# Second-layer weights and last-stage factors requested by ScalarE in a queue of its own

## The chip, the core and the metric

The kernel runs on one core of a Trainium2 chip. Its engines are TensorE (PE in the profile), VectorE (DVE), ScalarE (ACT), GpSimd (POOL) and SyncE (SP); 16 DMA engines move data between the memory off the core (DRAM) and the on-chip buffers. The metric is the device time of one execution in microseconds (us): the median of three runs before is 2799.62 us, the lowest 2792.89, the highest 2799.96.

## The reference, cut to what matters

One inference step of a two-layer decoder, for a prompt of 2048 positions and 32 sample positions, width 1024. The first layer is gated linear attention. The second is attention over a sliding window of 128 positions, with 32 query heads in four groups that share one key and value head each, a gate, and an output projection:

```
q, gate = split(rmsnorm(h) @ b_w_in)          # 1024 -> 2048 + 2048
q = rope(rmsnorm(q per head))
o = attend(q, k_p, v_p, sinks)                # blocks of 128 queries
h = h + (o * silu(gate)) @ b_w_out            # 2048 -> 1024
```

`k_p, v_p` are projected once, from the residual stream after layer 0.

## The kernel before

A product of full precision is made of three f16 products of high and low halves, so each weight is held as a pair of f16 tiles. During layer 0 the kernel converts the weights of layer 1 into such pairs and writes them to DRAM: `Unit.prepare` (L247) writes the tensors called `pre`, and `form_steps` (L857) writes seven factors `wf0` to `wf6`, out of which the last stage makes the output projection of two blocks at a time with seven products in place of eight.

Layer 1 runs over four groups of heads (g), in each over 16 blocks of 128 positions (c): 64 iterations n = 16 g + c, and three more in which the pipeline runs empty. An iteration does three things woven together by the string `ORDER` (L1526): the projections of block n ("f" stands for one of 24 steps, TensorE's filler), the scores of block n-2 ("A", four of them, two heads each) and the values of block n-3 ("B", two of them). The order of TensorE's instructions is pinned from L1525 on; on the other engines a scheduler sets it when the kernel is built, by when it believes each instruction to be ready. After it is set, each engine and each DMA queue works strictly in it.

Between scores and values stands a chain: VectorE takes the minimum (L1281), ScalarE takes exponentials (L1286) and the high half (L192), VectorE the low half (L193), and SP's queue turns the result round with a DMA transposition into the buffers `sth` (heads 0, 1, 4, 5 of the group) and `pst` (heads 2, 3, 6, 7) at L1289, which the values read. SP's queue also holds the transposition of the queries (`X<-qe`, L1245), that of the output (`og<-ogT`, L638) and its store (`oge<-og`, L639), and the load of keys and values (`gl<-KVd`, L1233): some eight to eleven requests in an iteration.

In the same queue of SP stand the requests that the change touches, 64 of 512 KB each:

- `W<-pre` (L267, `Unit.fetch`), 36 of them: the prepared weights, four for keys and values, and eight for each group (four for the queries, four for the gate). They go into a ring of 12 buffers `W` (`NW`).
- `W<-wf` (L1542, `wform`), 12: factors 3, 4 and 5, into the same ring.
- `uT<-wf` (L1537, `wform_big`), 16: factors 0, 1, 2 and 6, a quarter each, into buffers `uT`.

The eight requests of the next group are traced at the end of iteration c = 12 (L1726). The scheduler moved them: it placed each where it believed the buffer free. A DMA request counts on one of eight semaphores that all requests of SP and ScalarE share in turn, so a request also waits until the last one that had the same semaphore, some eight requests back, has landed.

Of the kernel before, what the change touches and what calls it, by code (L numbers as in the profile page):

```python
# [22 lines left out]
NCH = SEQ // P  # L23
# [5 lines left out]
NKV = 4  # L29
# [35 lines left out]
def build(tc, i, o):  # L65
    nc = tc.nc
    ctx = ExitStack()
    with ctx:
        cp = ctx.enter_context(tc.tile_pool(name="cp", bufs=1))
        sb = ctx.enter_context(tc.tile_pool(name="sb", bufs=2))  # L70
        ps = ctx.enter_context(tc.tile_pool(name="ps", bufs=1, space=PSUM))
        dr = ctx.enter_context(tc.tile_pool(name="dr", bufs=1, space=DRAM))
        _body(tc, nc, cp, sb, ps, dr, i, o)


def _body(tc, nc, cp, sb, ps, dr, i, o):
# [6 lines left out]
    def T(tag, shape, dt, bufs=None):  # L83
        return sb.tile(shape, dt, tag=tag, name=nm(tag), **({} if bufs is None else {"bufs": bufs}))
# [22 lines left out]
    def later(dst, src, q=nc.sync):  # L107

        tc.keep_in_program_order(q.dma_start(dst, src))
# [31 lines left out]
    wfd = [dr.tile([P, 8, 2, 512], F16, tag=f"wf{n}", name=f"wf{n}") for n in range(7)]  # L141
# [17 lines left out]
    def run(steps):  # L159
        for f in steps:  # L160
            f()
# [39 lines left out]
    class Unit:  # L201
# [62 lines left out]

        def fetch(self):
            self.t = T("W", [P, 2, 1024], F16, NW)
            nc.sync.dma_start(self.t, self.pre)  # L267

        def __call__(self, k, hl, s):
            return self.t.rearrange("p z (k c) -> p z k c", c=self.ncol)[:, hl, k, s]  # L270
# [582 lines left out]
    gw = [GroupW(g) for g in range(NKV)]  # L853
# [677 lines left out]
    def wform_big(n, x, box={}):  # L1531

        if x == 0:
            t = box[n] = T("uT", [P, 8, 2, 512], F16, 4)
            wf[n] = lambda k, hl, s=ALL: t[:, k, hl, s]
        ks = slice(2 * x, 2 * x + 2)
        nc.sync.dma_start(box[n][:, ks], wfd[n][:, ks])  # L1537

    def wform(n, x, ts={}):

        t = ts[n, x] = T("W", [P, 2, 2, 512], F16, NW)
        nc.sync.dma_start(t, wfd[n][:, 2 * x : 2 * x + 2])  # L1542
        wf[n] = lambda k, hl, s=ALL: ts[n, k // 2][:, k % 2, hl, s]

    quarters = lambda f, n: [lambda x=x: f(n, x) for x in range(4)]
# [140 lines left out]
    def s_out(half):  # L1686

        cols = [slice(z * P, (z + 1) * P) for z in range(4)]
        right = [k + 2 for k in UP]
        fs, kts = ((0, 2, 5), UP + UP + right) if half else ((0, 3), UP + right)  # L1690
        return out_sample([lambda k, hl, z=z: wf[fs[k // 8]](k % 8, hl, z) for z in cols], half, b_finish_s, kts, OSCB)

    for t in range(-3, NKV * NCH):
        fill = []
        n = t + 3
        if n < NKV * NCH:
            g, c = divmod(n, NCH)
            blk = BBlk(g, c, gw[g])
            fill = blk.steps()
            parts[n] = blk.attend_steps()  # L1700
            if c == (SMC if g + 1 < NKV else 0):
                sm = SampleB(g, gw[g])
                boundary += [lambda sm=sm: run(sm.proj_steps())] + sm.steps()
        elif n < NKV * NCH + 3:
            fill = (pairs[0].steps(0) + pairs[0].steps(1), pairs[1].steps(0) + pairs[1].steps(1), s_out(0) + pairs[0].steps(2))[n - TOT]
        lists = {
            "A": list(parts[t + 1][0]) if t + 1 in parts else [],
            "B": list(parts.pop(t)[1]) if t in parts else [],
        }
        nf = ORDER.count("f")  # L1710
        seen = done = 0
        for x in ORDER:
            if x == "f":
                seen += 1
                upto = len(fill) * seen // nf
                run(fill[done:upto])
                done = upto
                if trickle and seen % 3 == 0:
                    trickle.pop(0)()
                if boundary and seen == 7 and n > TOT - NCH + 3:  # L1720
                    boundary.pop(0)()
                if summing and seen % 6 == 3 and (n > TOT or seen > 12):
                    summing.pop(0)()
            elif lists[x]:
                lists[x].pop(0)()
        if n < NKV * NCH and c == 12:  # L1726
            if g + 1 < NKV:
                run(gw[g + 1].steps())
        if n == TOT - 11:
            t_ = T("uT", [P, 8, 8, P], F16, 4)  # L1730
            for x in range(4):
                pr = pairs[x // 2]
                pr.l[x % 2] = [t_[:, 2 * x], t_[:, 2 * x + 1]]
                if x < 2:
                    pr.r[x] = pr.l[x]
                pr.fetch(x % 2, pr.l[x % 2])
        if n in (TOT - 7, TOT - 4):
            run(quarters(wform_big, {TOT - 7: 0, TOT - 4: 2}[n]))
        if n == TOT - 14:
            run(quarters(wform, 3))  # L1740
        if n == TOT - 1:
            trickle += [lambda x=x: pairs[0].load(x) for x in (3, 2)] + quarters(wform_big, 1)
            summing += pairs[0].sums()
        if n == TOT:
            trickle += quarters(wform, 4) + quarters(wform, 5)
        if n == TOT + 1:
            trickle += quarters(wform_big, 6)
        if boundary:
            boundary.pop(0)()
# [3 lines left out]
    for p_ in range(NCH // 2):  # L1753
# [8 lines left out]
        if p_ in (3, 4):  # L1762
            n = p_ - 3
# [87 lines left out]
```

## Time and profile before

| | us |
|---|---|
| median of 3 runs | 2799.62 |
| lowest and highest | 2792.89 and 2799.96 |
| the profiled execution, whole | 2794.24 |
| its span, first to last instruction | 2792.4 |
| TensorE busy in the span | 2700.0 (97%) |
| VectorE, ScalarE, GpSimd busy | 1701.5, 1391.9, 1134.0 |
| mean granted TensorE clock | 0.991 |

The profile comes from one execution with the hardware profiler on. "Busy" is the time in which an engine has an instruction under way. A view of windows gives, for a stretch of the span, the busy time of each engine (instructions in brackets), then the granted clock of TensorE, the mean busy share of the 16 DMA engines (which can pass 1, since an engine can have two packets under way) and the rate. A view of waits gives what an engine waited for in its idle time. A timeline gives start and duration of instructions, equal ones that follow each other as one row ("x12"), and in square brackets how long the engine was idle before and what released it. "SPq" and "ACTq" are requests: their duration is the time that the engine takes to issue them, not that of the transfer.

### The profile page before, as it was taken

The numbers are of one execution on the slowest core, as the hardware profiler recorded it, in microseconds if no ns is written. First come the engines' busy times: TensorE is split into PE (matmuls) and PEld (weight loads), VectorE is DVE, ScalarE is ACT, GpSimd is POOL, SyncE is SP. The second block draws the span as 40 slices with busy tenths as digits, with TensorE's granted clock in tenths as the row PEclk, the third lists the DMA queues.
The fourth block names the chain that finished last, engine by engine and source line by source line (L and its number), as shares of the span: only waits on it lengthen the run. The fifth ranks groups of instructions, "written<-read, shape, count | busy, mean of one in ns | idle before, by whom it ended". The sixth has DMA issues, their size and how long they took to land.

```text
span 2792.4 us, 51853 instructions
## 1 busy us (share of the span) xinstructions
PE 2700.0 (97%) x19266; PEld 1384.8 (50%) x19266; DVE 1701.5 (61%) x3474; ACT 1391.9 (50%) x3245; POOL 1134.0 (41%) x1604
## 2 busy tenths in 40 slices
PE   6899999999999999999999999999999999989999
PEld 4444544544454444445444555555555555544444
DVE  5655665666667564446413656677777767777653
ACT  6554655555556554433313555566666666651110
POOL 2342233322433231126305676666667657530000
PEclk9999999999999999999999999999999999999999
DMA  8462444433434454789846778978978889896431
GB/s 213 92 149 55 105 115 125 110 106 103 135 107 115 115 168 121 227 252 295 245 160 155 131 155 154 230 131 158 198 136 153 178 168 186 171 223 200 151 103 58
DMA packets 814470, 429.53 MB, mean 154 GB/s; under 512 B 649600, under 2 KB 723144, under 8 KB 814184
## 3 DMA queue, kind: packets, MB, share of 16 engines
q1 hardware_dynamic: 801256, 390.49, 59.8%
q0 software_dynamic: 10880, 35.66, 3.6%
q8 instruction: 150, 2.46, 0.4%
q14 instruction: 104, 0.85, 0.1%
q10 hardware_dynamic: 2080, 0.07, 0.0%
HBM read 178.75 MB, written 107.54 MB: 103 GB/s over the span
## 4 chain that ended last, share of the span: by engine, by line
PE 65%; ACT 9%; DMA 9%; DVE 7%; issue 5%; POOL 5%; SPq 1%; ACTq 0%; POOLq 0%; DVEq 0%
PE pj L102 39%; PE o L102 12%; PE tr L102 10%; PE kv L102 3%; ACT o L1286 2%; DMA pst<-v 2%; PE lev L102 1%; DVE v L193 1%; ACT v L192 1%; DMA wraw<-in_a_w_in_dram 1%; DMA pre<-pst 1%; DMA W<-in_state_gla_dram 1%; DVE o L1281 1%; POOL ogT L190 1%; DVE lev L1281 1%
## 5 line engine op out<-in xcount | busy, mean ns | idle before, releaser
L102 PE MATMUL pj<-W,uT 128*128 128x512 f16 x5088 | 1196.9, 380 | 6.9 <-ACT sg L500 2.5
L102 PEld LDWEIGHTS <-uT 128*128 128x128 f16 x6976 | 649.9, 98 | 697.5 <-issue 20.8
L102 PE MATMUL tr<-W,uT 128*128 128x512 f16 x1536 | 365.5, 379 | 0.0
L102 PEld LDWEIGHTS <-X 128*128 128x128 f16 x2744 | 184.6, 98 | 140.9 <-issue 9.9
L1286 ACT ACTIVATE o<-o,mx 128x256 f32<-128x256 f32 (+1 forms) x384 | 168.7, 439 | 166.7 <-DVE mx L1281 161.1
L181 POOL TENSOR_SCALAR rs_m<-ss 128x1 f32<-128x1 f32 (+3 forms) x190 | 43.6, 230 | 496.0 <-DVE ss L1183 184.2
L102 PE MATMUL pj<-uT,W 128*128 128x512 f16 (+1 forms) x912 | 189.3, 357 | 26.9 <-DMA uT<-ogT 23.9
L1281 DVE CUSTOM_DVE_ANT_0 o<-o,madd,nsink 128x256 f32<-128x256 f32 (+1 forms) x384 | 183.9, 479 | 43.5 <-PE o L102 39.2
L193 DVE SCALAR_TENSOR_TENSOR v<-o,v 128x512 f16<-128x512 f32 (+1 forms) x192 | 128.9, 672 | 104.6 <-ACT v L192 102.1
L182 POOL TENSOR_TENSOR rs_r<-rs_m,mhalf 128x1 f32<-128x1 f32 (+2 forms) x186 | 186.9, 1005 | 14.1
L533 POOL TENSOR_TENSOR KQ<-KQ,bt 128x256 f32<-128x256 f32 x112 | 99.9, 892 | 227.7 <-DVE X L190 222.4
L102 PEld LDWEIGHTS <-W 128*128 128x128 f16 x2448 | 129.9, 99 | 114.8 <-issue 23.0
L102 PEld LDWEIGHTS <-v 128*128 128x128 f16 x976 | 95.2, 98 | 115.7 <-issue 2.3
L190 POOL TENSOR_TENSOR ogT<-og,ogT 128x512 f16<-128x512 f32 x68 | 83.7, 1232 | 125.7 <-ACT ogT L189 120.6
L189 ACT ACTIVATE X<-KQ 128x512 f16<-128x512 f32 x128 | 84.6, 661 | 84.6 <-PE lev L102 61.1
L102 PEld LDWEIGHTS <-sg 128*128 128x128 f16 x800 | 77.7, 98 | 93.4 <-issue 1.2
L102 PE MATMUL o<-gl,X 128*128 128x256 f16 (+1 forms) x768 | 113.5, 270 | 7.6 <-DMA X<-qe 3.6
L192 ACT ACTIVATE v<-o 128x512 f16<-128x512 f32 (+1 forms) x192 | 111.2, 579 | 3.5
L190 DVE TENSOR_TENSOR X<-KQ,X 128x512 f16<-128x512 f32 x128 | 98.2, 767 | 21.2 <-ACT X L189 19.7
L1286 ACT ACTIVATE lev<-lev,mx 128x256 f32<-128x256 f32 (+1 forms) x128 | 56.5, 441 | 104.8 <-DVE mx L1281 102.8
L396 POOL TENSOR_TENSOR bt<-bt 128x256 f32<-128x256 f32 (+6 forms) x112 | 46.5, 416 | 146.5 <-ACT bt L385 139.5
L259 POOL DMA_DIRECT2D pre<-pst x72 | 50.4, 703 | 133.5 <-DVE pst L193 109.4
(439 smaller groups left out, 4871.1 us busy)
## 6 DMA issues: line engine op xcount, KB each, us to landing
pre<-pst POOLq DMA_DIRECT2D x72, 256.0 KB, 3.7
W<-pre SPq DMA_DIRECT2D x36, 512.0 KB
ogd<-ogk SPq DMA_DIRECT2D x68, 256.0 KB
wraw<-in_a_w_in_dram SPq DMA_DIRECT2D x64, 256.0 KB
wraw<-in_b_w_in_dram SPq DMA_DIRECT2D x64, 256.0 KB
oge<-og SPq DMA_DIRECT2D x64, 256.0 KB
wraw<-in_a_w_out_dram SPq DMA_DIRECT2D x32, 256.0 KB
X<-in_x_prompt_dram SPq DMA_DIRECT2D x32, 256.0 KB
```

The source lines that it names most:

```text
L102: return order(nc.tensor.matmul(*a, **k))
L181: pool.tensor_scalar(m[:n, :k], ss, a, b, ALU.mult, ALU.add)
L182: pool.tensor_tensor(r[:n, :k], m[:n, :k], mhalf[:n, :k], ALU.pow)
L189: act(hi, src, AF.Copy)
L190: eng.tensor_tensor(lo, src, hi, ALU.subtract)
L192: put(act(hi, src, AF.Copy, scale=sc))
L193: dve.scalar_tensor_tensor(lo, src, sc, hi, ALU.mult, ALU.subtract)
L259: nc.gpsimd.dma_start(self.pre[:, :, half * 512 : half * 512 + 512], t)
L396: pool.tensor_tensor(dst, two[:, :, 0], two[:, :, 1], ALU.mult)
L533: pool.tensor_tensor(keys, keys, d[:, :, 1:2].to_broadcast([P, NB, m]), ALU.mult)
L1281: dve.tensor_tensor_reduce(pm[:, z], pm[:, z], madd.rearrange("p a b -> p (a b)")[:, (2 - nk) * P :], -0.125, nsink[:, g * GRP + h : g * G ...
L1286: act(pm[:, z], pm[:, z], AF.Exp, scale=-1.0, bias=nm_[:, h : h + 1], accum_out=bx["sum"][:, h : h + 1])
```

## The change

The three places that request prepared data call `later(..., nc.scalar)`, a helper that stands in the kernel already (L107). It issues the request on the given engine, here ScalarE, and pins it behind what was traced on that engine before it. The place of the group requests in the code changes too: four at the end of iteration c = 12, the other four in iteration c = 15 after filler steps 15, 17, 19 and 21.

```diff
         def fetch(self):
             self.t = T("W", [P, 2, 1024], F16, NW)
-            nc.sync.dma_start(self.t, self.pre)
+            later(self.t, self.pre, nc.scalar)
...
         ks = slice(2 * x, 2 * x + 2)
-        nc.sync.dma_start(box[n][:, ks], wfd[n][:, ks])
+        later(box[n][:, ks], wfd[n][:, ks], nc.scalar)
...
         t = ts[n, x] = T("W", [P, 2, 2, 512], F16, NW)
-        nc.sync.dma_start(t, wfd[n][:, 2 * x : 2 * x + 2])
+        later(t, wfd[n][:, 2 * x : 2 * x + 2], nc.scalar)
...
+                if n < NKV * NCH - NCH and c == NCH - 1 and seen in (15, 17, 19, 21):
+                    nextg.pop(0)()
...
-        if n < NKV * NCH and c == 12:
-            if g + 1 < NKV:
-                run(gw[g + 1].steps())
+        if n < NKV * NCH - NCH and c == 12:
+            nextg = gw[g + 1].steps()
+            run(nextg[:4])
+            del nextg[:4]
```

Three places show how the built order moves. The first is SP's queue in the last iteration of group 0, from the output's transposition on; `W` are the weight buffers, `KVd`, `out_cvp` and `out_ckp` stores of keys and values. Before:

```order
L267 DMA W_18853<-pre_173 128x2048
L267 DMA W_18855<-pre_174 128x2048
L639 DMA oge_118<-og_19374 512x1x256
L267 DMA W_18857<-pre_175 128x2048
L1245 DMA_TRANSPOSE X_19388<-qe_19385 128x8x128
L267 DMA W_18859<-pre_176 128x2048
L1289 DMA_TRANSPOSE sth_19423<-v_19411 128x8x128
L1212 DMA KVd_15341<-w_3205_19454 512x1x128
L267 DMA W_18861<-pre_177 128x2048
L1224 DMA out_cvp_dram<-E_19470 128x256
```

And now:

```order
L639 DMA oge_118<-og_19366 512x1x256
L1245 DMA_TRANSPOSE X_19380<-qe_19377 128x8x128
L1289 DMA_TRANSPOSE sth_19415<-v_19403 128x8x128
L1212 DMA KVd_15341<-w_3201_19446 512x1x128
L1224 DMA out_cvp_dram<-E_19462 128x256
```

The weight requests are gone from between SP's own, and the rest stands as it did. Twelve stood here before (`pre_173` to `pre_184`: group 1's eight, and group 2's first four, whose buffers come free at the same time); the eight of group 1 now stand on ScalarE in this iteration.

The second place is ScalarE at the end of iteration 28 (g = 1, c = 12), behind the gate's activation; `qe` is the queries' high half, `Sh` a tile of the sample positions, `o` the scores, `es` the sink's exponential. Before:

```order
L1237 ACTIVATE sg_22576<-tr_22486 128x512
L1454 ACTIVATE Sh_22604<-tr_22595 128x1024
L1310 ACTIVATE es_3717_22641<-es_3717_22641 128x8
L189 ACTIVATE qe_22567<-KQ_22479 128x8x64
L1286 ACTIVATE o_22609,sm_3712_22607<-o_22609,mx_22606 128x256 x2
```

And now:

```order
L1237 ACTIVATE sg_22576<-tr_22486 128x512
L109 DMA W_22579<-pre_181 128x2048
L109 DMA W_22581<-pre_182 128x2048
L109 DMA W_22583<-pre_183 128x2048
L109 DMA W_22585<-pre_184 128x2048
L189 ACTIVATE qe_22567<-KQ_22479 128x8x64
L1454 ACTIVATE Sh_22596<-tr_22587 128x1024
L1286 ACTIVATE o_22601,sm_3708_22599<-o_22601,mx_22598 128x256
```

Group 2's first four requests moved 13 iterations back, from the end of group 0 to here, and stand in a row ahead of the exponentials. Such a row of four stands at four more places: group 3's first four at the end of iteration 44, factor 3 after iteration 50, factor 0 after 57, factor 2 after 60.

The third place is the run-out, from iteration 64 on, in SP's queue before; `E<-hd` loads the residual stream.

```order
L1542 DMA W_30765<-wf_127 128x2048
L1542 DMA W_30808<-wf_127 128x2048
L1633 DMA E_30724<-hd_134 128x512
L1542 DMA W_30837<-wf_127 128x2048
L1542 DMA W_30844<-wf_128 128x2048
L1289 DMA_TRANSPOSE pst_30403<-v_30391 128x8x128
L1542 DMA W_30874<-wf_128 128x2048
L1542 DMA W_30930<-wf_128 128x2048
L1289 DMA_TRANSPOSE sth_30447<-v_30435 128x8x128
```

The same requests on ScalarE now:

```order
L192 ACTIVATE v_30817<-o_30818 128x512
L189 ACTIVATE ke_30631<-wraw_30810 128x512
L189 ACTIVATE X_30753<-wraw_30628 128x512
L109 DMA W_30765<-wf_127 128x2048
L109 DMA W_30808<-wf_127 128x2048
L109 DMA W_30837<-wf_127 128x2048
L109 DMA W_30844<-wf_128 128x2048
L1286 ACTIVATE lev_30857,sm_5009_30731<-lev_30857,mx_30730 128x256
```

Factors 4 and 5 moved from ahead of factor 1, around the end of iteration 63, to iteration 65: the numbers of the scores beside them (`v_30391` there, `v_30817` here) show it.

## The prediction

> **What bounds the kernel now.** I read the page first, for the engine that fills the span:
>
> ```profile
> PE 2700.0 (97%) x19266; PEld 1384.8 (50%) x19266; DVE 1701.5 (61%) x3474; ACT 1391.9 (50%) x3245; POOL 1134.0 (41%) x1604
> ```
>
> TensorE is busy 2700.0 of 2792.4 us; only its idle 92 us, and the time in which its clock is low, can be won without taking work from it. Then the windows, at places where second-layer requests stand, with one quiet stretch (2050 to 2075):
>
> ```profile
> 1750.00:1800.00 50.00, 44.79 (x386) 24.65 (x384) 29.62 (x79) 26.68 (x77) 28.21 (x40) 1.00 1.08 260
> 2000.00:2025.00 25.00, 23.17 (x233) 13.22 (x233) 19.78 (x55) 17.00 (x51) 14.57 (x18) 1.00 1.14 265
> 2050.00:2075.00 25.00, 25.00 (x296) 15.45 (x295) 17.07 (x46) 14.83 (x45) 13.20 (x18) 1.00 0.74 131
> 2225.00:2250.00 25.00, 20.94 (x192) 11.11 (x190) 18.84 (x53) 15.89 (x48) 15.28 (x19) 0.93 1.13 264
> 2350.00:2375.00 25.00, 23.52 (x200) 13.31 (x199) 18.23 (x49) 15.20 (x46) 13.58 (x19) 1.00 1.08 219
> 2425.00:2450.00 25.00, 23.09 (x204) 13.34 (x203) 17.78 (x45) 13.79 (x40) 12.62 (x15) 1.00 0.93 165
> 2450.00:2475.00 25.00, 21.93 (x169) 12.25 (x168) 15.75 (x38) 12.88 (x38) 13.02 (x17) 0.93 0.99 259
> 2475.00:2500.00 25.00, 19.24 (x135) 10.30 (x134) 19.81 (x44) 12.58 (x33) 2.60 (x4) 0.93 1.08 241
> ```
>
> Behind a window's bounds and length stand the busy times of PE, PEld, DVE, ACT and POOL, then the clock, the DMA engines' share and GB/s. In the quiet stretch TensorE loses nothing and the DMA engines are 0.74 busy. Where requests stand they are at 0.93 to 1.14, and TensorE loses 5.2, 1.8, 4.1, 1.5, 1.9, 3.1 and 5.8 us: 23.4 us in all. That is the stake. The view of TensorE's waits says for what it stood:
>
> ```profile
> PE pj L102 <- DMA uT<-ogT: 23.9, 7, 16.8
> PE kv L102 <- DMA pst<-v: 14.5, 6, 4.3
> ...
> PE o L102 <- DMA X<-qe: 3.6, 3, 2.0
> PE o L102 <- DMA gl<-KVd: 3.4, 1, 3.4
> ```
>
> The first row is layer 0's. The other three, 21.5 us, are layer 1's transpositions and key loads: never a weight, always something that stands behind weights in SP's queue. SP's timeline shows how they stand there:
>
> ```profile
> 1754.98 1.01 SPq L267 DMA_DIRECT2D W<-pre  x2
> ...
> 1769.39 3.16 SPq L1228 DMA_TRANSPOSE og<-lvm  x1
> 1772.65 1.01 SPq L267 DMA_DIRECT2D W<-pre  x2
> 1773.75 0.39 SPq L1233 DMA_DIRECT2D gl<-KVd  x1
> 1774.22 3.16 SPq L1289 DMA_TRANSPOSE sth<-v  x1
> ...
> 1780.88 0.53 SPq L267 DMA_DIRECT2D W<-pre  x1
> ...
> 1991.25 1.05 SPq L267 DMA_DIRECT2D W<-pre  x2
> ...
> 2011.98 0.53 SPq L267 DMA_DIRECT2D W<-pre  x1
> ...
> 2217.94 1.06 SPq L267 DMA_DIRECT2D W<-pre  x2
> ...
> 2234.72 0.52 SPq L1542 DMA_DIRECT2D W<-wf  x1
> ```
>
> Twelve requests stand from 1755.0 to 1781.4, eight from 1991.3 to 2012.5, eight from 2217.9 to 2235.2 (the first and last of each are shown). A weight costs SP 0.5 us to issue, but the transposition behind it takes 3.16 us to go out.
>
> **What one request costs.** From 1750 to 1800 the rate is 260 GB/s against 131 in the quiet stretch: 129 times 50 us is 6.45 MB, just the twelve requests (12 times 0.524 MB). The share is 0.34 higher: 17 us of all 16 engines, 1.4 us for each. A quiet stretch leaves 0.26 of the engines free. How much lag does TensorE stand? In a quiet iteration the `pst` transposition that the first values read goes out at 2433.64 and is read at 2441.17, from SP's and TensorE's timelines:
>
> ```profile
> 2433.64 1.51 SPq L1289 DMA_TRANSPOSE pst<-v  x1
> ```
>
> ```profile
> 2441.17 0.51 PE L102 MATMUL kv<-gl,pst 128*128 128x64 f16 x12
> ```
>
> That is 7.5 us, of which 1.5 are the issue and some 2 I estimate for landing: a cover of 4 us. So a stall is the work of the requests, less what the free share takes meanwhile, less 4. Twelve in 26.4 us: 17 - 6.9 - 4 = 6.1 (measured 5.2). Eight in 21.2: 11.3 - 5.5 - 4 = 1.8 (measured 1.8). Eight in 17.3: 11.3 - 4.5 - 4 = 2.8 (measured 4.1). The fours of factors 0 and 2 come out at nothing and cost 1.5 and 1.9: two requests right ahead of a transposition hurt it more than the average says.
>
> **The change part by part.** SP's queue loses 64 requests. The group starts keep eight, four and four on ScalarE in place of twelve, eight and eight; group 2's and 3's first fours go to iterations 28 and 44, factor 3 to 50. With the same formula: group 1's eight spread over the same 26 us give 11.3 - 6.9 - 4 = 0.4; the fours at the other two starts, spread over some 8 us, give 5.6 - 2.1 - 4, nothing. Each row of four, issued within some 2 us, gives 5.6 - 0.5 - 4 = 1.1, and there are five of them: 5.5. The Trainium skill ("DMA: Bandwidth & Descriptors", section "Queues, rings and completion order") says that a DMA engine takes its queues in turn, packet by packet, so that long packets of weights would pass ahead of most of the transpositions' short ones; by it I estimate 5.6 - 4 = 1.6 for a row of four and a sum smaller by 2.5 us. No row of this trace has two such queues busy. So the 14.5 us of the first five windows with loss become 5.9: a gain of 8.6. The first twelve requests of the layer cost nothing in either form, as TensorE is still at the first layer's products and ScalarE has little to do.
>
> In the run-out twelve requests stood close together around the start of iteration 64; now factor 1's four go out in 64 and the eight of factors 4 and 5 in 65, so the first stall below loses most of its cause and the second keeps it:
>
> ```profile
> 2471.42 0.82 PE L102 MATMUL kv<-gl,pst 128*128 128x64 f16 x12 [3.07 <-DMA pst<-v]
> 2472.05 1.90 PE L102 MATMUL pj<-uT,uT 128*128 128x512 f16 x4
> ...
> 2482.78 3.62 PE L102 MATMUL pj<-uT,uT 128*128 128x512 f16 x16
> 2487.87 0.51 PE L102 MATMUL kv<-gl,sth 128*128 128x64 f16 x12 [1.48 <-DVE wraw L1325]
> 2492.66 0.82 PE L102 MATMUL kv<-gl,pst 128*128 128x64 f16 x12 [4.28 <-DMA pst<-v]
> ```
>
> Of the 8.8 us I take 2 off, no more, since eight requests still have to pass in one iteration, and the 1.48 us are VectorE's. The rows show a second price: behind a stall of 3 us TensorE runs at half speed (four products in 1.90 us, where sixteen take 3.62), about 1.8 us more each. I count 1.8 us for one such stall gone.
>
> ScalarE takes 64 requests. Its only two in this trace, at the start, are these:
>
> ```profile
> L128 ACTq DMA_DIRECT2D gsa<-in_a_norm_dram x1: 471/471/471, 0.7 to 0.7; - x1
> ```
>
> ```profile
> L342 ACTq DMA_DIRECT2D E<-in_a_w_in_dram x1: 600/600/600, 1.2 to 1.2; - x1
> ```
>
> At 0.47 to 0.60 us, 64 take 30 to 38 us of an engine that is 14.8 of 25 us busy in a quiet window. A row of four holds back what is queued behind it by about 2.2 us: the queries' half, the exponentials, and so VectorE, SP's transpositions and TensorE's values. That lies within the same cover of 4 us, but spends it together with the lag; without the cover it would be 2.2 at each of five rows, 11 us. I charge 2.
>
> Sum: 8.6 + 2 + 1.8 - 2 = 10.4 us. The profiled execution, 2794.24 us, would become 2783.8. The median of the runs shown stands 5.4 us above it; taking the gain from the median gives 2789 us, 0.37% less. A measurement of this kernel can tell about 0.3% (8.4 us) from no change.
>
> **Rivals.** First, the load only moves. All transfers still go over the same 16 engines, and the windows above say that they are full where TensorE waits. If lag is lag, whoever's queue holds the request, the small transfers then wait on engines instead of in the queue, the rows of four cost what the scattered fours cost (five times 1.7, 8.5), the starts keep a third of their loss (3.7), the run-out keeps all: 14.5 - 12.2 - 2 for ScalarE is a gain of 0.3: 2799. For it speaks that the formula, which knows nothing of queues, meets three of five stalls; against it the fours that it misses, which only the order in the queue explains. The Trainium skill ("DMA: Bandwidth & Descriptors", section "Issuing engines are not separate DMA queues") speaks for it: requests of all engines run on the same DMA engines and interleave, and another issuer saves only issue time.
>
> Second, slower: ScalarE is held up at the request. SP's transpositions grow from 1.51 to 3.16 us when the path behind the queue is full. If a request of ScalarE is held by that path too, each takes some 0.5 + 1.65 us, and a row of four 8.6. Less the cover of 4, each of the five rows costs 4.6 us, 23 in all, and the run-out's eight another 5; with the starts' 0.4 that is 28.4 in place of 14.5, so 2813. It decides from about 2 us for a request on ScalarE; at 1.5 us the rows of four cost 10, the run-out 2, and the gain shrinks to 2. The same end is reached if a request waits long for the semaphore it shares with SP's. For it: ScalarE is in order and feeds the chain that TensorE waits on. Against it: plain requests on SP stayed at 0.5 us in the full stretches.
>
> Third, the separate queue frees SP's transpositions altogether: all of 14.5, most of the run-out's 7.4 us of DMA waits, both slow clocks (3.6), less 2: 23 us, 2776.
>
> **How the numbers follow.** My forecast (a gain of 4 to 16 us) has 0.40, no change 0.27, held-up ScalarE or another new stall 0.18, everything freed 0.10, and 0.05 is something else, mostly no change. Of the forecast's band about three quarters, 0.31, pass 8.4 us; with the third rival and a little of the rest this makes 0.43 faster. Same gets 0.09, 0.27 and 0.03: 0.39. Slower 0.18. The range reaches to the third rival's 2776 below and to 2806 above, where most of the slower cases begin.
>
> **What would show it.** Right: at the three group starts TensorE's windows lose under 1 us each; transpositions at L1289 go out in 1.2 to 1.6 us there; at the five rows of four on ACTq a request takes about 0.5 us and TensorE loses about 1 us behind each; the first slow stretch near 2471 is gone. Wrong: requests on ACTq of 2 us and more, TensorE waiting on ScalarE's exponentials or on `pst<-v` behind each row of four by 3 us and more, or on a weight itself; and for the first rival, the same total of waits on `pst<-v`, `X<-qe` and `gl<-KVd` as now, spread over more places.

## The result, and the profile after

The changed kernel takes 2815.42 us (median of 7 runs, 2806.60 to 2824.46) where the kernel before takes 2799.62. The ratio is 1.0053, with an interval of 1.0034 to 1.0073: 15 us slower, where 10 us faster was forecast. Its profiled execution took 2821.64 us, with a span of 2819.8, 27.4 longer than that of the kernel before.

The first line of the page after, with all five engines:

```profile
PE 2707.4 (96%) x19266; PEld 1385.6 (49%) x19266; DVE 1695.0 (60%) x3474; ACT 1392.0 (49%) x3245; POOL 1137.1 (40%) x1604
```

TensorE's same 19266 products take 7.4 us more, and some 20 us more are idle. Most of the 7.4 us is time at a lower granted clock: summed over windows of 10 us, busy time times the missing share of the clock comes to 24.8 us after and 18.6 before. The windows after, at the places of the prediction and some more (columns as there; the dots stand for the windows between):

```profile
1475.00:1500.00 25.00, 20.79 (x91) 8.84 (x89) 5.97 (x11) 5.36 (x11) 10.99 (x16) 0.93 0.97 201
1750.00:1800.00 50.00, 38.23 (x305) 19.91 (x304) 20.78 (x54) 20.91 (x60) 25.59 (x37) 0.86 0.95 176
1975.00:2000.00 25.00, 23.18 (x196) 12.98 (x195) 19.30 (x56) 17.21 (x51) 15.48 (x19) 1.00 1.04 211
2000.00:2025.00 25.00, 25.00 (x249) 14.53 (x248) 19.28 (x49) 16.82 (x52) 16.52 (x23) 1.00 0.97 206
2200.00:2225.00 25.00, 23.77 (x220) 13.52 (x218) 18.72 (x56) 16.84 (x48) 15.78 (x19) 1.00 1.03 200
2225.00:2250.00 25.00, 25.00 (x238) 14.34 (x237) 18.77 (x50) 16.44 (x50) 16.31 (x22) 1.00 0.95 211
2350.00:2375.00 25.00, 24.97 (x225) 14.48 (x224) 18.78 (x48) 16.54 (x47) 16.31 (x19) 1.00 1.02 189
2425.00:2450.00 25.00, 25.00 (x215) 14.35 (x212) 18.98 (x49) 15.61 (x45) 14.54 (x18) 1.00 0.95 221
...
2500.00:2525.00 25.00, 15.92 (x205) 10.91 (x205) 22.32 (x47) 12.39 (x31) 6.31 (x6) 0.73 0.88 194
2525.00:2550.00 25.00, 17.87 (x127) 8.64 (x125) 5.50 (x10) 1.43 (x3) 0.00 (x0) 0.84 1.17 253
```

The last two of these in the kernel before:

```profile
2500.00:2525.00 25.00, 22.82 (x279) 14.28 (x278) 14.24 (x28) 6.84 (x18) 4.50 (x5) 0.93 0.89 244
2525.00:2550.00 25.00, 25.00 (x118) 11.33 (x116) 23.27 (x39) 6.19 (x10) 0.00 (x0) 1.00 0.66 197
```

Half of the forecast is there: the starts of groups 2 and 3 (2000 and 2225) lose nothing, the first two rows of four lose 1.8 and 1.2 us (1975 and 2200), and the stalls near 2350 and 2440 are gone. Three places lose instead: 4.2 us at the layer's first weights (1475, nothing before), 11.8 at group 1's start (1750 to 1800, 5.2 before), and the run-out, 16.2 us in its last two windows (2.2 before); over all of 2450 to 2550 it is 22.2 against 11.0.

Three rows divide layer 1 into stretches: ScalarE's last pass over layer 0 (L320), its one `es<-es` per iteration (L1310) and SP's one store of an iteration's result (L639). Before, and then after (first and last start stand behind the durations):

```profile
L320 ACT ACTIVATE og<-st x17: 613/629/631, 1144.1 to 1473.8; 128x512 bf16<-128x512 f32 x16, 32x512 bf16<-32x512 f32 x1
...
L1310 ACT ACTIVATE es<-es x64: 191/212/226, 1519.1 to 2503.8; 128x8 f32<-128x8 f32 x64
...
L639 SPq DMA_DIRECT2D oge<-og x64: 520/534/1445, 1545.7 to 2529.7; - x64
```

```profile
L320 ACT ACTIVATE og<-st x17: 613/629/631, 1147.9 to 1476.7; 128x512 bf16<-128x512 f32 x16, 32x512 bf16<-32x512 f32 x1
...
L1310 ACT ACTIVATE es<-es x64: 191/208/228, 1527.9 to 2515.9; 128x8 f32<-128x8 f32 x64
...
L639 SPq DMA_DIRECT2D oge<-og x64: 527/534/912, 1554.9 to 2557.6; - x64
```

The first weights (L320's last to the first `es`) went from 45.3 to 51.2 us, the loop (first to last `es`) from 984.7 to 988.0, the run-out (last `es` to the last store) from 25.9 to 41.7. Layer 0, which the change doesn't touch, ended 2.9 us later. The waits of TensorE after:

```profile
PE lev L102 <- DVE v L193: 8.3, 1, 8.3
PE o L102 <- DMA X<-qe: 8.3, 3, 4.8
PE kv L102 <- DMA pst<-v: 7.8, 4, 3.9
PE pj L102 <- DVE KQ L1187: 6.9, 1, 6.9
...
PE pj L102 <- DMA W<-pre: 4.2, 2, 3.7
PE kv L102 <- DVE wraw L1325: 3.7, 1, 3.7
```

The waits on `pst<-v` are about halved (14.5 to 7.8), but a few long ones came instead, two of them on VectorE (8.3 us in the run-out, 6.9 at group 1). At group 1's start TensorE stands twice:

```profile
1785.01 1.04 PE L102 MATMUL o<-gl,X 128*128 128x256 f16 x4 [4.85 <-DMA X<-qe]
1792.97 6.12 PE L102 MATMUL pj<-W,uT 128*128 128x512 f16 x16 [6.92 <-DVE KQ L1187]
```

What stands behind that is seen on SP's queue and on ScalarE (its third to fifth request; the first two are at 1762.29 and 1763.59):

```profile
1762.90 1.52 SPq L638 DMA_TRANSPOSE og<-ogT  x1
1779.21 0.53 SPq L639 DMA_DIRECT2D oge<-og  x1
1779.84 1.44 SPq L1245 DMA_TRANSPOSE X<-qe  x1
```

```profile
1764.88 1.62 ACTq L109 DMA_DIRECT2D W<-pre  x2
1779.58 0.33 ACTq L109 DMA_DIRECT2D W<-pre  x1
1779.95 0.42 ACT L189 ACTIVATE lvm<-E 128x256 f16<-128x256 f32 x1 [9.09 <-DMA W<-pre]
1788.71 0.60 ACT L1182 ACTIVATE E<-pj 128x512 f32<-128x512 f32 x1 [8.34 <-DMA out_cvp_dram<-E]
```

A request costs ScalarE only 0.33 us. But the transposition that SP asked for at 1762.90 has its store only at 1779.21, 16 us later, and SP asks for nothing in between. Both waits of TensorE follow from that. The transposition of the queries (`X<-qe`) stands behind that store in SP's order and goes out at 1779.84: the first 4.85 us. A store `out_cvp_dram<-E`, three requests after it, goes out only at 1784.71, and ScalarE can't write its next `E` until it has landed: the 8.34 us above, which VectorE and TensorE pass on as the 6.92.

ScalarE's own fifth request waits too, 9.09 us. It has the semaphore of ScalarE's second one (1763.59), because all requests of SP and ScalarE take turns on eight, and that one had not landed. This wait lies beside the chain: neither stall of TensorE leads back to it. In the run-out a second such wait, of 7.34 us, does lead to one of TensorE's, of 2.55 us out of 22. More than half of the 22 us, a wait of 3.74 and one of 8.28, leads back to a load `qe<-oge`, for which VectorE stood:

```profile
2498.85 0.69 DVE L1591 TENSOR_TENSOR wraw<-S,qe 128x512 f32<-128x512 f16 x1 [10.23 <-DMA qe<-oge]
```

The load stands in SP's queue behind a transposition that took 12.8 us to land, beside three weights of ScalarE's; it took 12.1 us itself, 4.3 in the kernel before.

The DMA queues from 1764 to 1778, and in the kernel before over its twelve requests (1754 to 1782; queue, packets, MB, share of 16 engines):

```profile
DMA packets 1880, 2.25 MB, mean 161 GB/s; under 512 B 1417, under 2 KB 1417, under 8 KB 1877
...
q10 hardware_dynamic: 510, 1.88, 74.7%
q1 hardware_dynamic: 1367, 0.33, 30.4%
```

```profile
DMA packets 10293, 8.13 MB, mean 290 GB/s; under 512 B 8157, under 2 KB 8925, under 8 KB 10289
...
q1 hardware_dynamic: 10289, 8.08, 110.8%
```

By busy share the engines are full in both, but with weights in ScalarE's queue (q10) beside transpositions in SP's (q1) they move 161 GB/s, with all in SP's queue 290.

### The profile page after: what moved, and what is told of

Its sections match the earlier page's. It is cut to its first block, busy times and chain, and to the rows that moved or that the text cites. A ratio compares the mean times of both kernels' runs of the same rounds, so it can differ in the third digit from the quotient of the medians.

```text
span 2819.8 us, 51816 instructions
## 1 busy us (share of the span) xinstructions
PE 2707.4 (96%) x19266; PEld 1385.6 (49%) x19266; DVE 1695.0 (60%) x3474; ACT 1392.0 (49%) x3245; POOL 1137.1 (40%) x1604
## 4 chain that ended last, share of the span: by engine, by line
PE 65%; DMA 12%; ACT 6%; issue 6%; DVE 5%; POOL 4%; SPq 1%; ACTq 0%; POOLq 0%; DVEq 0%
PE pj L102 38%; PE tr L102 12%; PE o L102 9%; PE kv L102 4%; PE lev L102 2%; DMA W<-in_state_gla_dram 1%; DMA pst<-v 1%; DMA KQ<-in_b_w_out_dram 1%; DMA wraw<-in_a_w_in_dram 1%; DMA wraw<-in_a_w_out_dram 1%; DMA out_st_s_dram<-W 1%; POOL ogT L190 1%; POOL rs_r L182 1%; DMA pre<-pst 1%; ACT o L1286 1%
## 5 line engine op out<-in xcount | busy, mean ns | idle before, releaser
L102 PEld LDWEIGHTS <-X 128*128 128x128 f16 x2744 | 184.7, 98 | 146.7 <-DMA X<-qe 12.1
```

Of the source, the lines that this page charges most:

```text
L102: return order(nc.tensor.matmul(*a, **k))
```

## The experiments

Three theories stood at the start. Theory Q: the second queue loses. Theory P: the new places of the requests lose. Theory S: what is lost is ScalarE's time for 64 requests. In the diffs below `later(dst, src)` without an engine uses SP's queue.

**e1_place_sp**, the changed places in SP's queue (likewise at L1537 and L1542):

```diff
-            later(self.t, self.pre, nc.scalar)
+            later(self.t, self.pre)
```

> The changed kernel with one thing put back: all 64 requests stand at the changed places, pinned there, but in SyncE's queue. Theory Q (the second queue loses: a request in ScalarE's queue and a transposition in SyncE's slow each other, and the semaphores they share make both in-order engines wait): the stalls of the changed kernel near 1785-1793 and 2505-2547 go, no wait of TensorE on W<-pre near 1490, the rows of four cost 1 to 2 us each, and the time is 4 to 10 us under the kernel before, some 2792. Theory P (the places lose: rows of four inside an iteration, the run-out's twelve later than before): as slow as the changed kernel, 10 to 16 us over the kernel before, some 2812, with the same stalls at the same places. Theory S (64 requests' time on ScalarE): 15 us under the changed kernel, but spread, with the waits on pst<-v as long as in the changed kernel.

Measured: 2812.48 us, a ratio to the kernel before of 1.0039 [1.0026, 1.0052]. The run-out takes 28.6 us and the first weights 46.1, close to the kernel before (25.9 and 45.3), so those two losses belong to the queue. But the loop takes 997.0, and at group 1 TensorE waits on weights themselves, which stand pinned among SP's other requests (1750 to 1810; over the whole loop 13.5 us):

```profile
PE tr L102 <- DMA W<-pre: 7.4, 3, 6.5
```

Theory Q alone is not enough: the changed places, in SP's queue, lose 12 us in the loop. For them P holds, but not "with the same stalls".

**e2_old_place_act**, the queue alone (the two edits to the order of requests undone):

```diff
-        if n < NKV * NCH - NCH and c == 12:
-            nextg = gw[g + 1].steps()
-            run(nextg[:4])
-            del nextg[:4]
+        if n < NKV * NCH and c == 12:
+            if g + 1 < NKV:
+                run(gw[g + 1].steps())
```

> The queue alone: all 64 requests in ScalarE's queue, but each group's eight asked for together at the group's start (iterations 28 and 44 get no rows of four). Theory Q: the losses of the changed kernel at the first weights (4 us), at group 1 and in the run-out (11 us of waits) stay, groups 2 and 3 start with eight in a row and lose some 5 us each like group 1; 15 to 30 us over the kernel before, some 2820. Theory P: the time of the kernel before within 5 us. Theory S: as the changed kernel within 4 us, since the number of requests is the same.

Measured: 2831.02 us, 1.0110 [1.0094, 1.0126]; loop 998.1, run-out 35.7, first weights 46.5. That is theory Q's direction and slightly more than its 15 to 30 us, but the first weights lost only 1 us of the 4 it expected. Theory S falls: the same number of requests, 16 us apart. In this profile ScalarE has no wait for a weight's semaphore at group 1, and TensorE stands 10.3 us there all the same; `out_cvp_dram<-E` holds ScalarE for 11.1.

**e3_pre_only** and **e4_wf_only**, one half of the change each (L267, or L1537 and L1542, back to `nc.sync.dma_start`; in e4 the places of the prepared weights too).

> Half of the change: the 36 prepared weights in ScalarE's queue at the changed places, the 28 requests of the factors in SyncE's queue as before. Theory Q: the run-out is as in the kernel before (idle of TensorE from 2450 to 2550 some 11 us instead of 22), the losses at the first weights and group 1 stay, the gains at groups 2 and 3 too: within 6 us of the kernel before, 2797 to 2806. Theory P: as theory Q for the run-out. Theory S: a gain against the changed kernel of 28/64 of 15 us, 7 us, spread over the whole layer and not in the run-out.

> The other half: the 28 requests of the factors in ScalarE's queue, the prepared weights in SyncE's as before. Theory Q: the first weights and group 1 as in the kernel before, the run-out as in the changed kernel (22 us of idle from 2450 to 2550 and half-speed stretches), the rows of four near 2350 and 2440 gain 3 us: 8 to 15 us over the kernel before, some 2811. Theory S: 28/64 of 15 us over the kernel before, 7 us, spread.

Measured: e3 2807.39 us, 1.0024 [1.0012, 1.0036], first weights 53.3, loop 988.2, run-out 25.9. e4 2810.41 us, 1.0034 [1.0019, 1.0049], first weights 45.2, loop 978.3, run-out 43.9. Each loss goes with the requests that stand there. (e3 came out 7 us over the kernel before, 1 us outside theory Q's range.)

**e5_all_pool**, the changed places in GpSimd's queue, which has eight semaphores of its own:

```diff
-            later(self.t, self.pre, nc.scalar)
+            later(self.t, self.pre, nc.gpsimd)
```

> The changed kernel with all 64 requests in GpSimd's queue at the same places. GpSimd's requests take turns on eight semaphores of their own, ScalarE's and SyncE's on eight common ones. Theory Q1 (the common semaphores make ScalarE and SyncE wait for each other's landings): from the last es<-es of ScalarE (L1310) to the last oge<-og of SyncE (L639) the run-out takes 26 to 30 us as in the kernel before (25.9) instead of 41.7 in the changed one, ScalarE has no 7 to 9 us of idle for a DMA, the group 1 start loses under 6 us: 0 to 6 us over the kernel before. Theory Q2 (a second queue beside SyncE's slows the transpositions on the 16 engines, whoever holds it): run-out 38 us or more, group 1 as in the changed kernel: 10 to 20 us over the kernel before.

Measured: 2860.39 us, 1.0229 [1.0207, 1.0251]; first weights 45.3, loop 1016.3, run-out 40.2. Neither theory forecast so much, and the first weights lost nothing. TensorE's largest waits in the loop are on the transposition of the queries (8.3 us in the changed kernel):

```profile
PE o L102 <- DMA X<-qe: 30.9, 7, 7.0
```

GpSimd itself stands 15.3 us at requests whose buffers aren't free; what that adds isn't separated. For the run-out the answer is plain. GpSimd's requests, SP's queue and TensorE:

```profile
2543.14 2.16 POOL L109 DMA_DIRECT2D uT<-wf  x4
```

```profile
2544.13 11.79 SPq L1289 DMA_TRANSPOSE pst<-v  x1
```

```profile
2559.15 0.82 PE L102 MATMUL kv<-gl,sth 128*128 128x64 f16 x12 [7.62 <-DMA sth<-v]
```

SP's request for a transposition, 1.24 us at the median of this line, takes 11.79 beside four weights of another queue. The common semaphores aren't needed for the loss (Q1 falls); a second queue beside SP's is enough (Q2).

**e6_three_factors**, **e7_mix** and **e8_mix_sp**: first the kernel before with factors 3, 0 and 2 alone in ScalarE's queue; then with the prepared weights of groups 2 and 3 there too (factors 1, 4, 5 and 6 keep `nc.sync.dma_start`); then e7's places in SP's queue.

```diff
         def fetch(self):
             self.t = T("W", [P, 2, 1024], F16, NW)
-            nc.sync.dma_start(self.t, self.pre)
+            if self.by_act:
+                later(self.t, self.pre, nc.scalar)
+            else:
+                nc.sync.dma_start(self.t, self.pre)
...
+            for f in nextg:
+                f.__self__.by_act = g > 0
+            now = 4 if g else 8
```

> The kernel before, with only the factors 3, 0 and 2 (twelve requests in rows of four) in ScalarE's queue at their changed places; the run-out's sixteen and all 36 prepared weights as before. If the run-out's loss is all of the second half's, the loop keeps its 6 us (first to last es<-es 978 us against 984.7), the run-out takes 26 us again: 3 to 7 us under the kernel before, some 2795. If the loop's gain in the run before this was chance: within 3 us of the kernel before.

> What the segments point to: ScalarE's queue for the prepared weights of groups 2 and 3 and for factors 3, 0 and 2 at their changed places; the first twelve, group 1's eight and the run-out's sixteen in SyncE's queue as before. Group 1's start then holds eight requests instead of twelve (in the kernel before four of group 2's were there): by the forecast's formula 6.1 us less 1 to 2; groups 2 and 3 gain 3 us: 8 to 12 us under the kernel before, some 2790, and from the first to the last es<-es 972 to 977 us. If each request in ScalarE's queue costs what the changed kernel's excess is, 15 us over 64, then 28 of them cost 7 us and it is no faster than the kernel before.

> The same places as in e7_mix, with the 28 requests pinned in SyncE's queue. If it is the queue that gains in the loop (transpositions no longer stand behind weights), this is 5 to 10 us slower than e7_mix, near the kernel before, and SyncE's transpositions behind the rows of four go out in 3 us instead of 1.3. If it is the place alone (spread requests), it equals e7_mix within 3 us.

Measured: e6 2795.54 us, 0.9994 [0.9980, 1.0009], no difference. The loop took 988.7 us here and 978.3 in e4 with nearly the same requests in it, so the loop's length from one profiled execution is good to some 10 us, and e6's own profiled execution (2810.81) lies 15 us above its median. e7 2791.18 us, **0.9970 [0.9958, 0.9981]**, the only version faster than the kernel before; first weights 45.2, loop 974.1, run-out 26.2. e8 2809.87 us, 1.0042 [1.0027, 1.0058], loop 988.6. TensorE's waits from 1950 to 2350, e7 and then e8:

```profile
PE kv L102 <- DMA pst<-v: 2.1, 3, 1.1
PE o L102 <- DMA X<-qe: 1.6, 2, 0.9
```

```profile
PE kv L102 <- DMA pst<-v: 4.9, 3, 3.3
PE tr L102 <- DMA W<-pre: 4.5, 2, 2.5
PE kv L102 <- DMA sth<-v: 3.9, 2, 2.5
```

At the same places these requests cost 3.7 us in ScalarE's queue and 13.3 in SP's, and the medians differ by 18.7, more than the 5 to 10 expected. There the prediction's idea holds: in one queue transpositions stand behind the row's first weights, and its last weights behind transpositions. (e8 pins its requests among SP's, so it isn't the kernel before with other places.)

**e9_side_by_side** and **e10_when_starved** measure the disputed cost by itself, behind the last product, when nothing else runs.

```diff
+        [("w", x, S_) for x in range(4)] + [("t", x) for x in range(4)],
...
+        [("w", x, A_) for x in range(4)] + [("t", x) for x in range(4)],
```

> The kernel before, and behind its last product, with nothing else on the chip, nine small stages of three repetitions each, parted by VectorE: four transpositions of 128x1024 in SyncE's queue; four weights of 512 KB there; four weights, then four transpositions there; the two in turn there; four weights in ScalarE's queue beside four transpositions in SyncE's; the same with GpSimd's queue; two weights in ScalarE's queue beside the four; eight weights in SyncE's queue; four in ScalarE's beside four in SyncE's. Its output is the reference's, its time some 300 us longer. Theory M (long and short packets side by side cost both queues bandwidth, as 161 GB/s at group 1's start of the changed kernel beside 290 at the kernel before's): one queue takes about the sum, 5 us for the transpositions and 6 for the weights, 11 to 13 us; two queues take 14 to 20 us, GpSimd's as ScalarE's, and the transpositions land last; eight weights take the same 11 to 12 us in one queue or two. Theory N (the packets share 16 engines without loss; what delays is ScalarE's and SyncE's order and their common semaphores): two queues take 9 to 13 us, no more than one, and the first transposition lands 2 to 4 us after the start.

> As e9_side_by_side, the kernel before with small stages behind its last product, three repetitions of each: four weights in ScalarE's queue beside one transposition; three beside four; four beside four that were asked for 2 us ahead of them; four beside four that come 2 us behind them; two, then two more 6 us later, beside four; four beside four that come one by one, some 3 us apart; the last in SyncE's queue alone. In e9 four beside four took 15.5 to 17.7 us instead of 12.6 and the first transposition landed 12.7 to 15.1 us after the start, two beside four took 10.3 with the first at 6.6. Theory D (the number decides: beyond two weights in the air the transpositions starve): three and four lose, whenever they come, also the one by one (first landing behind 10 us); two and two do not (first at 7). Theory O (what was asked for first is served first): with the transpositions 2 us ahead the first lands after 3.4 to 5 us and nothing is lost; with them 2 us behind the first lands 8 to 10 us after its own request. Theory L (only a pile of transpositions loses bandwidth): one transposition beside four weights lands within 9 us, and one by one the stage takes 13 us as in SyncE's queue.

One repetition of e9 with all in SP's queue, and one with the weights in ScalarE's; VectorE's rows show when each transposition had landed:

```profile
2877.14 1.86 SPq L1791 DMA_DIRECT2D W<-wf  x4
2879.09 1.80 SPq L1794 DMA_TRANSPOSE sth<-v  x1
...
2886.56 0.16 DVE L1785 COPY lvm<-sth 128x1 f16<-128x1 f16 x1 [8.97 <-DMA sth<-v]
...
2889.99 0.16 DVE L1785 COPY lvm<-pst 128x1 f16<-128x1 f16 x1 [1.05 <-DMA pst<-v]
...
2974.47 1.78 ACTq L1791 DMA_DIRECT2D W<-wf  x4
2974.95 1.23 SPq L1794 DMA_TRANSPOSE sth<-v  x1
...
2987.76 0.16 DVE L1785 COPY lvm<-sth 128x1 f16<-128x1 f16 x1 [12.83 <-DMA sth<-v]
...
2990.48 0.16 DVE L1785 COPY lvm<-pst 128x1 f16<-128x1 f16 x1 [1.06 <-DMA pst<-v]
```

All stages by such rows, three repetitions each (us from a stage's first request to its last landing, and to the first transposition's, unless the row says otherwise; "the four" are four transpositions in SP's queue):

| stage | whole | first transposition |
|---|---|---|
| four transpositions, SP | 7.3, 7.3, 7.3 | 3.4, 3.2, 3.3 |
| four weights, then four transpositions, SP | 12.6, 12.6, 12.8 | 9.2, 9.3, 9.4 |
| the same in turn, SP | 13.9, 14.3, 14.2 | 5.4, 5.4, 5.4 |
| four weights on ScalarE beside the four | 17.7, 15.5, 16.0 | 15.1, 12.7, 13.3 |
| four weights on GpSimd beside the four | 12.7, 15.6, 15.5 | 6.7, 13.1, 12.6 |
| two weights on ScalarE beside the four | 10.3, 10.5, 10.4 | 6.9, 7.1, 7.0 |
| eight weights, SP / four and four in two queues | 14.0, 13.9, 14.2 / 13.7, 13.7, 13.6 | |
| e10: four weights on ScalarE beside one | | 11.7, 11.1, 13.0 |
| e10: transpositions one by one, four weights on ScalarE / SP | 17.8, 18.8, 16.1 / 13.3, 13.6, 13.3 | |
| e10: the first of four transpositions 2.7 us ahead of four weights on ScalarE | 18.0, 17.9, 18.2 | 3.2; the third 14.4 after its own request |
| e10: the first of four transpositions 2.7 us behind four weights on ScalarE | 13.9, 12.6, 13.1 | 7.8, 6.5, 7.1 after its own request |

Theory M holds and N falls: two queues of weights share the engines without loss, but weights beside transpositions cost some 3 us in all (with GpSimd in two of three repetitions). Beside four weights in ScalarE's queue the first transposition, asked for within 0.5 us of the first weight, lands after 11 to 15 us; it takes 3.3 alone and 9.3 behind the same weights in one queue.

Of e10's three theories none holds whole. One transposition is enough (L falls). Three weights starve it too (10.8 to 13.2 us), and two, with two more 8.1 us later, gave 9.2 to 10.8, so two aren't always safe either (against D). Of the four transpositions ahead of the weights, the first two went out 2.7 and 1.4 us before the first weight and landed after 3.2 us each, as O says; the third went out with the first weight and took 14.4, so the stage lost some 5 us all the same. Those 2.7 us behind the first weight, and over 1 us behind the last, landed after 6.5 to 7.8 us, where O expected 8 to 10, and the stage lost little.

**e11_mix_group1**, e7 with group 1's eight in ScalarE's queue (`by_act = True`, `now = 4`).

> e7_mix with one thing more in ScalarE's queue: group 1's eight prepared weights at their changed places; the first twelve and the run-out stay in SyncE's queue. Theory M (what the small stages showed: weights in a second queue starve a transposition asked for at the same time, 11 to 16 us instead of 3.3): the loop from the first to the last es<-es takes 986 to 990 us as in the changed kernel and e3_pre_only (988), against 974.1 in e7_mix, with TensorE's waits at X<-qe or KQ near 1785; the first weights and the run-out as in e7_mix; 10 to 14 us slower than e7_mix, some 2803. If group 1's loss in the changed kernel came from what its first twelve left late, the loop takes 974 to 978 us and the time is e7_mix's.

Measured: 2799.60 us, 0.9992 [0.9979, 1.0005], 8 us slower than e7 (10 to 14 expected); loop 990.6, first weights and run-out as in e7. The stall of the changed kernel comes back in the same form, and again the chain behind it runs over `og<-ogT` (16.2 us) and `out_cvp_dram<-E`, not over ScalarE's wait for a semaphore (8.26 us this time):

```profile
1780.46 1.04 PE L102 MATMUL o<-gl,X 128*128 128x256 f16 x4 [4.98 <-DMA X<-qe]
1788.79 5.45 PE L102 MATMUL pj<-W,uT 128*128 128x512 f16 x16 [7.29 <-DVE KQ L1191]
```

## Why the prediction was wrong

The forecast was a gain of 10.4 us; a loss of 15 came. The step that failed is the price of a request in a second queue, at group 1 and in the run-out. By the prediction's steps:

- **The rows of four, 1.1 us each.** Right: 1.8, 1.2 and 0.6 us at 1975, 2200 and 2275, about nothing at the last two (near 2391 and 2435). The lag behind it was longer than forecast. The trace counts landings on each request's semaphore, and by these counts `pst` landed after 9.2 to 12.3 us at the five rows, where the median transposition of layer 1 takes 3.4: 6 to 9 us more, where 5.1 was forecast. Less the cover of 4 this would leave 2 to 5; TensorE lost less, so the cover must be wider than 4 us at most rows.
- **The starts of groups 2 and 3, nothing.** Right, and with e8 against e7 the reason too: the transpositions no longer stand behind weights in their queue.
- **Group 1's eight, 0.4 us.** This step failed. It took for each request 1.4 us of all 16 engines, whichever queue holds it, and let a transposition wait only for what the free share couldn't take: a lag of 4.4 us. But beside weights of another queue the rate fell from 290 to 161 GB/s, and one transposition took 16 us. The cover of 4 us doesn't reach over that; besides, it was read from `pst` alone, and the chain here ran over `og<-ogT` and `X<-qe`. The windows show 11.8 us of idle and a clock of 0.86; e11 shows that this start alone costs 8 us of the time.
- **The layer's first twelve, nothing in either form.** Failed in part: 51.2 and 53.3 us instead of 45.3 in two profiled executions, 46.5 in a third (e2). The last four weights came late, and TensorE waited on them, 3.7 and 0.6 us. GpSimd's queue lost nothing there (45.3, e5), so why ScalarE's did stays open.
- **The run-out, 2 us off.** Failed by the same step as group 1: it counted how many requests stand close together, not which transpositions of another queue stand beside them. In seven kernels with these requests in SP's queue the run-out took 25.9 to 28.6 us, in four with another queue 35.7 to 43.9.
- **ScalarE's 64 requests, 2 us.** The requests are mostly cheaper than the 0.47 to 0.60 us assumed (0.33 at the median of `W<-pre`, 0.39 and 0.45 for the factors). ScalarE stood in two long waits for a shared semaphore, 9.09 us at group 1 and 7.34 in the run-out, but only the second reached TensorE, with 2.55 us: the size of the term was about right, for another reason.

The second rival gave 2813 us and came near in the time, but its mechanism was mostly another: a request isn't held 2 us each. Its last sentence, that a request may wait long for the semaphore it shares with SP's, did occur, as a consequence: a landing has to be late first. It explains little of the loss: group 1 stalls nearly as long without it (10.3 us in e2, 11.8 after), and the run-out takes 40.2 us without it (e5). That the time came near 2813 is luck.

The prediction weighed a rule of the Trainium skill ("DMA: Bandwidth & Descriptors", section "Queues, rings and completion order"): a DMA engine takes its queues in turn, packet by packet. The trace agrees in so far as both queues move on: in 14 us q10 gets 510 long packets through and q1 1367 short ones, not one for one. The size doesn't follow from it: by turns, I estimate, four weights and a transposition would be through in about the 9.2 us of one queue, and it took 11.1 to 13.0. The Trainium skill (the same page, section "Issuing engines are not separate DMA queues") says that another issuer saves only the time to issue. For plain loads e9 agrees (14.0 and 13.7 us). Beside transpositions the runs don't agree with the "only": the same places differ by 19 us between e8 and e7 in favour of the second queue, and in the run-out by 13 against it (28.6 in e1, 41.7 in the changed kernel).

What stays open is by what rule a transposition is passed. By the counts of landings, one that was asked for between the first weight and two or three more took 10.5 to 16.2 us in the stages, one asked for behind the last weight 6.3 to 7.8. In the changed kernel it is alike: `og<-ogT` at group 1 stood behind the first of four requests (16.3 us), and `pst` at the third row of four in the middle of the row (12.3); at the other four rows `pst` was asked for behind the last request (9.2 to 10.0). But in e2 `og<-ogT` stood behind the first request in the same way and landed after 5.2 us, so this order isn't the whole rule, and no run varied it alone.

## What to carry to other kernels

Transfers in two queues aren't independent when one of them carries DMA transpositions. Here moving bulk loads out of the transpositions' queue paid at rows of four whose transposition had some us of cover, and lost where the next transposition, or what stands behind it in its queue, was needed at once; there the loads did better in the same queue. Try such a change place by place, since one edit can gain in one stretch and lose in the next; here the good half was worth 0.3% and the whole cost 0.5%. A request in a compute engine's queue can hold up that engine until an earlier request with the same semaphore has landed, here 9.09 and 7.34 us, not its own 0.33. But follow the chain before blaming the longest wait: the 9.09 us cost TensorE nothing, and a store that stood late in another queue cost it 6.92.

## What the runs showed of the hardware

- With four 512 KB loads asked for by ScalarE within some 2 us, a 128x1024 transposition in SP's queue landed after 11.1 to 15.1 us instead of 3.2 to 3.4 alone and 9.2 to 9.4 behind them in one queue; asked for 2.7 us behind the first of them it took 6.5 to 7.8.
- Eight 512 KB loads took 14.0 us in one queue and 13.7 in two: without transpositions a second queue made no difference of note.
- The engines' busy share doesn't show the loss: 0.95 at 176 GB/s after, 1.08 at 260 before, in the windows from 1750 to 1800.
